# Moving the per-layer embeddings' projections out of the feed-forwards and into the mixers

## The chip, the cores and the metric

The program runs on one core of one Trainium2 chip. The metric is device time in microseconds (us) of one execution of the whole program. Lower is better.

## What is computed

The reference applies two stacks of two layers each to 256 tokens of width 1024. The first stack (feed-forward, mixer, memory attention, feed-forward) is not touched by the change. The second stack does this for its two layers `i`, with `layer_norm` after each step:

```python
h = layer_norm(DN_ALPHA * h + 0.5 * swiglu(h, ffn_w1[i, 0], ffn_w3[i, 0], ffn_w2[i, 0]), ...)
if i % 2 == 0:   # short convolution and state space
    mix = concat([ya, yb]) @ ab_w_out[j]
else:            # sparse attention
    mix = dsa_mixer(h @ c_w_in[j], ...) @ c_w_out[j]
h = layer_norm(DN_ALPHA * h + mix, ...)
h = layer_norm(DN_ALPHA * h + 0.5 * swiglu(h, ffn_w1[i, 1], ffn_w3[i, 1], ffn_w2[i, 1]), ...)
h = h + (p[i] @ ple_w_proj[i]) * jax.nn.sigmoid(h @ ple_w_gate[i])
```

The product `p[i] @ ple_w_proj[i]` is the projection that moves. It is 256 tokens by 256 by 1024, it depends on inputs alone, and it is wanted only in the last line of a layer.

## The kernel before, in words

Tokens are handled in two tiles of 128 (`T` = 0 and 1). Each float32 product is made as three matmuls in a reduced format: high part by high part, high by low, low by high (`mm3`, lines 147 to 152). So each weight that is loaded into a buffer `raw` is split by ScalarE (`whi`, line 126) and VectorE (`wlo`, line 127) before TensorE uses it. There are three `raw`, five `whi` and five `wlo` buffers for the whole program. SyncE's queue issues the weight loads.

A feed-forward (`ffn`, line 293) walks over eleven slices of the hidden width. The last three slices' products with `w_down` form its tail: first all of `T` = 0, then all of `T` = 1. Behind each tile's tail comes `ln_fin`, the layer norm (`L955` to `L578` on VectorE, with one small instruction on GpSimd), and `prep`, which transposes the normalised rows on TensorE (`xT`, `L177`) and splits them into the next stage's operands. The tail of `T` = 1 covers the layer norm of `T` = 0. The layer norm of `T` = 1 is covered by the next stage's matmuls on `T` = 0.

In the second feed-forward of each layer, `pre_tail` calls `ple_proj` (line 964) ahead of the tail. It stages one weight (1 MB), loads each token tile's 128 rows of `p` into one buffer `pn` (`L974`, on ScalarE's DMA queue; `bufs=1`, so the second load waits for the first tile's transposes), transposes and splits them, makes 12 matmuls of 512 columns for each tile, and copies the results to `pr` on VectorE (`L980`). The tiles `pr`, `ph`, `plo` and `pn` are in a pool `pr0` or `pr1` that is opened before that feed-forward and closed after `ple`.

Each stage opens a pool of its own for its working tiles and closes it at its end; the layer norm's gain and bias rows are in that pool too. A stage's pool is laid over the memory of the pool that was closed before it. The state space stage (`ab_mixer`, line 1369) opens a pool, and issues on ScalarE's queue the loads of `NT` (two of 1 MB, `L1380`) and `tab` (768 KB, `L1382`). Then it projects `u` with `proj` (one pass over each token tile, 24 matmuls each) and goes on with products that need both tiles. The sparse attention (`dsa`, line 1000) projects its index queries, then keys and values, then queries, and then runs 16 pairs of head and token tile through scores, softmax, transposes and products with the values.

The framework orders the instructions of each engine when the program is built. An instruction that comes earlier in the program has precedence among those that it takes to be ready, and each engine then runs its own list in order.

Of the kernel before, what the change touches and what calls it, by code (L numbers as in the profile page):

```python
# [29 lines left out]
class Net:  # L30
# [116 lines left out]
    def mm3(self, out, xh, xl, wh, wl, first, last):  # L147
        nc = self.nc
        a, b = ((xl, wh), (xh, wl)) if self.opt("wlast") else ((xh, wl), (xl, wh))
        nc.tensor.matmul(out, xh, wh, start=first, stop=False)  # L150
        nc.tensor.matmul(out, *a, start=False, stop=False)  # L151
        nc.tensor.matmul(out, *b, start=False, stop=last)  # L152

    def both(self, out, ws, x2, n=8, parts=(0, 1)):

# [105 lines left out]
        return [self.stage([(0, w[h * 512:(h + 1) * 512, c0:c0 + width].rearrange("(k p) n -> p k n", p=P))], 4, width)  # L261
                for h in range(2)]

    def proj(self, preps, w, *chunks):

        ws = [self.stage_rows(w, c0, width) for c0, width, _ in chunks]
        for T in range(2):
            xh, xl = preps[T][0:2]
            for wc, (c0, width, cb) in zip(ws, chunks):
                pu = self.psum("A", "proj")  # L270
                for k in range(8):
                    wh, wl = wc[k // 4]
                    self.mm3(pu[:, 0:width], xh[:, k, :], xl[:, k, :], wh[:, k % 4, :], wl[:, k % 4, :], k == 0, k == 7)
                cb(T, pu)

    def out_linear(self, w, lhs, fin, tags=(("C", "C"), ("D1", "D2"))):

        ws = [self.stage([(0, w[i * 256:(i + 1) * 256, :].rearrange("(k p) n -> p k n", p=P))], 2, 1024) for i in range(4)]
        for T in range(2):
            acc = [self.psum(t, "acc") for t in tags[T]]  # L280
            if T and self.opt("halves"):
                order = [(k, n) for n in range(2) for k in range(8)]
            else:
                order = [(k, n) for k in range(8) for n in range(2)]
            for k, n in order:
                h, l = lhs(T, k)
                wh, wl = ws[k // 2]
                s = slice(n * 512, (n + 1) * 512)
                self.mm3(acc[n], h, l, wh[:, k % 2, s], wl[:, k % 2, s], k == 0, k == 7)
            fin(T, acc)  # L290


    def ffn(self, up_parts, w_down, fin, side=None, pooled=False, pre_tail=None, second=None, pieces=1):

        nc, tc = self.nc, self.tc
        (xh, xl), x2 = self.xT_cur, self.x2_cur
# [3 lines left out]
        with tc.tile_pool(name=self.nm("ffn"), bufs=2) as pool:  # L300
# [16 lines left out]
            def stage_down(c):  # L317
                return self.stage([(0, w_down[c * 256:(c + 1) * 256, :].rearrange("(k p) n -> p k n", p=P))], 2, 1024)
# [77 lines left out]
            if side is not None:  # L396
                for _ in side:
                    pass
            if pre_tail is not None:
                pre_tail()  # L400
            its = [(*ht, stage_down(c)) for c, ht in pend]
            for T in range(2):
                for halves in ((0,), (1,)) if T and self.opt("halves") else ((0, 1),):
# [560 lines left out]
    def ple_proj(self, l, pool):  # L964

        nc, a = self.nc, self.a
        pr = [pool.tile([P, D], F32, tag=f"pr{T}", bufs=1, name=self.nm("pr")) for T in range(2)]
        ph = pool.tile([P, 2, 256], F32R, tag="ph", bufs=1, name=self.nm("ph"))
        plo = pool.tile([P, 2, 256], F32R, tag="plo", bufs=1, name=self.nm("plo"))
        wh, wl = self.stage([(0, a["ple_w_proj_2"][l].rearrange("(k p) n -> p k n", p=P))], 2, 1024)  # L970
        for T in range(2):
            s = slice(T * P, (T + 1) * P)
            pn = pool.tile([P, 256], F32, tag="pn", bufs=1, name=self.nm("pn"))
            nc.scalar.dma_start(pn, a["p_2"][l, 0, T * P:(T + 1) * P, :])  # L974
            self.split_T(pn, 2, ph[:, :, s], plo[:, :, s])
            for n in range(2):
                pu = self.psum("A", "pp")
                for k in range(2):
                    self.mm3(pu, ph[:, k, s], plo[:, k, s], wh[:, k, n * 512:(n + 1) * 512], wl[:, k, n * 512:(n + 1) * 512], k == 0, k == 1)
                nc.vector.tensor_copy(pr[T][:, n * 512:(n + 1) * 512], pu)  # L980
        return pr

# [14 lines left out]
            self.out_linear(a["ple_w_gate_2"][l], lambda T, k: (preps[T][0][:, k, :], preps[T][1][:, k, :]), f)  # L997


    def dsa(self, fin):  # L1000
        nc, tc, a = self.nc, self.tc, self.a
        preps = self.preps()
        w_in = a["c_w_in_2"][0]
        with tc.tile_pool(name=self.nm("dsa"), bufs=1) as pl:
# [46 lines left out]
            def cb_q(c):  # L1051
                def cb(T, pu):
                    t = T_([P, 512], "tmp", bufs=2)
                    nc.scalar.activation(t, pu, AF.Copy, scale=128.0 ** -0.5)
                    rot(t.rearrange("p (h d) -> p h d", h=4), 4, T, 16, 16)
                    to_T(t, 4, qT[T][:, 4 * c:4 * c + 4, :])
                return cb
# [31 lines left out]
            for c in range(2):  # L1089
                self.proj(preps, w_in, (c * 512, 512, cb_q(c)))  # L1090

            oh, ol = self.o_tiles()
            for T in range(2):
                nk = P * (T + 1)
# [271 lines left out]
                    nc.sync.dma_start(self.d_mt[:, h, q, :], mt[:, 4 * h:4 * h + 4].rearrange("p g j c -> p (g j c)"))  # L1366


    def ab_mixer(self, fin):
        nc, tc, a = self.nc, self.tc, self.a  # L1370
        preps = self.preps()
        x2 = self.x2_cur
        w_in = a["ab_w_in_2"][0]
        with tc.tile_pool(name=self.nm("ab"), bufs=1) as pl:
# [12 lines left out]
            def cb_u(T, pu):  # L1387
# [3 lines left out]
                for j in range(4):  # L1391
                    nc.tensor.transpose(pt[:, j * P:(j + 1) * P], un[:, j * P:(j + 1) * P], self.ident)
                nc.vector.tensor_copy(uT[:, :, T * P:(T + 1) * P], pt.rearrange("p (k t) -> p k t", k=4))
            self.proj(preps, w_in, (1536, 512, cb_u))


            def projT(c0, cb, ws=None, qs=range(4)):
# [80 lines left out]
            for h in range(2):  # L1478
# [9 lines left out]
                for b in range(4):  # L1488
                    MT = T_([P, 4, P], "MT", bufs=4)
                    nc.sync.dma_start(MT.rearrange("p g m -> p (g m)"), self.d_mt[:, h, b])  # L1490
                    for mm in range(2):
                        n = 4 * b + 2 * h + mm
# [3 lines left out]
                        last = b == 3 and mm == 1  # L1496
# [22 lines left out]
            for q in range(4):  # L1519
                pu = self.psum("A", "glu")  # L1520
# [20 lines left out]
def build(tc, a, out):  # L1541
    with ExitStack() as ctx:
        net = Net(ctx, tc, a, out)
# [59 lines left out]
            net.ffn(net.gu_parts(a["ffn_post_w_gu"][l]), a["ffn_post_w_down"][l], f_next, side=None if l else net.s5_tables())  # L1603
        alpha = 4.0 ** 0.25
        for l in range(2):
            def f_ln(j, mul, eps):
                def f(T, acc, pool, *tags):
                    net.ln_fin(T, acc, mul, eps, l, j, pool, *tags)
                    net.prep(T, rms=False)
                return f  # L1610

            def f_end(T):
                if l == 0:
                    net.prep(T, rms=False)

            def ffn(half, j, **kw):
                net.ffn(net.w13_parts(a["ffn_w1_2"][l, half], a["ffn_w3_2"][l, half]), a["ffn_w2_2"][l, half],
                        f_ln(j, 2 * alpha, 4e-5), pooled=True, **kw)

            net.phase = f"ffn{l}0"  # L1620
            ffn(0, 0)
            net.phase = f"seq{l}"
            (net.ab_mixer if l == 0 else net.dsa)(f_ln(1, alpha, 1e-5))
            net.phase = f"ffn{l}1"
            with tc.tile_pool(name=f"pr{l}", bufs=1) as pp:
                pr = []
                ffn(1, 2, pre_tail=lambda: pr.extend(net.ple_proj(l, pp)))
                net.phase = f"ple{l}"
                net.ple(l, pr, f_end)

# [16 lines left out]
```

## Time and profile before

| | |
|---|---|
| median of 3 runs | 2262.38 us (2260.16 to 2263.03) |
| the profiled execution, its own time | 2264.35 us |
| span of the profiled execution | 2262.4 us |
| mean granted TensorE clock | 0.995 of full speed |
| TensorE matmul busy | 2212.8 us |
| VectorE busy | 1599.5 us |
| ScalarE busy | 1275.1 us |

Times in the views are counted from the span's start. The first feed-forward of layer 0 of the second stack ends and the state space stage begins at about 1430 us. The second feed-forward of that layer ends at about 1724 us. The sparse attention begins at about 1935 us, and the last feed-forward's tail at about 2209 us.

### The profile page before, as it was taken

How to read it: one execution, taken by the hardware profiler on the slowest of the kernel's cores; microseconds unless marked ns; L12 is line 12 of the kernel's file. 1: busy time of each engine (PE TensorE's matmuls, PEld its weight loads, DVE VectorE, ACT ScalarE, POOL GpSimd, SP SyncE). 2: the span in 40 equal slices, each digit the busy share in tenths (PEclk: the TensorE clock that was granted, in tenths of full speed). 3: DMA queues.
4: the chain of work that ended last, by engine and by line, in shares of the span. 5: the costliest groups of instructions: out<-in, count | busy, mean ns of one | idle time of the engine just before them, and what ended most of it. 6: DMA issues, size and time to landing. Idle time of an engine off the chain costs nothing.

```text
span 2262.4 us, 32375 instructions
## 1 busy us (share of the span) xinstructions
PE 2212.8 (98%) x11697; PEld 1844.3 (82%) x11697; DVE 1599.5 (71%) x3522; ACT 1275.1 (56%) x2864; POOL 71.1 (3%) x112
## 2 busy tenths in 40 slices
PE   8999999999999998999999999999999999999998
PEld 6887768788888886777888888787887888778887
DVE  7787666798766776776677565877568565967566
ACT  6745566655655566766555555364555555455553
POOL 0010000000000001100000000000000000000000
PEclk9999999999999999999999999999999999999999
DMA  7665534567577543343655655666555564527552
GB/s 240 228 215 196 191 127 168 161 213 264 177 220 247 173 155 118 130 162 120 200 171 187 223 174 198 219 198 216 185 187 186 187 201 159 166 94 245 186 184 79
DMA packets 280988, 415.94 MB, mean 184 GB/s; under 512 B 18662, under 2 KB 211324, under 8 KB 279804
## 3 DMA queue, kind: packets, MB, share of 16 engines
q1 hardware_dynamic: 275744, 400.87, 53.3%
q10 hardware_dynamic: 5084, 13.00, 1.6%
q8 instruction: 92, 1.51, 0.3%
q14 instruction: 68, 0.56, 0.1%
HBM read 400.07 MB, written 13.76 MB: 183 GB/s over the span
## 4 chain that ended last, share of the span: by engine, by line
PE 79%; DVE 11%; ACT 3%; DMA 2%; issue 2%; POOL 2%; SPq 0%; ACTq 0%; DVEq 0%; POOLq 0%
PE gate L160 11%; PE up L160 11%; PE acc L150 8%; PE acc L151 8%; PE acc L152 8%; PE gate L162 6%; PE up L162 6%; DVE wlo L127 4%; PE proj L151 2%; PE proj L150 2%; PE proj L152 2%; PE up L152 1%; PE up L151 1%; PE up L150 1%; PE xT L177 1%
## 5 line engine op out<-in xcount | busy, mean ns | idle before, releaser
L126 ACT ACTIVATE whi<-raw 128x512 fp32r<-128x512 f32 (+1 forms) x1452 | 816.5, 618 | 413.5 <-PE up L160 176.3
L127 DVE TENSOR_TENSOR wlo<-raw,whi 128x512 fp32r<-128x512 f32 (+1 forms) x1452 | 926.3, 675 | 107.1 <-ACT whi L126 69.6
L160 PE MATMUL gate<-x,whi 128*128 128x512 f32 x1200 | 295.1, 393 | 0.0
L160 PE MATMUL up<-x,whi 128*128 128x512 f32 x1200 | 290.6, 390 | 0.1
L150 PE MATMUL acc<-whi,hh 128*128 128x512 f32 x704 | 276.3, 392 | 2.0 <-ACT hh L192 2.0
L151 PE MATMUL acc<-wlo,hh 128*128 128x512 f32 x704 | 276.4, 393 | 0.0
L152 PE MATMUL acc<-whi,hl 128*128 128x512 f32 x704 | 275.1, 391 | 0.0
L167 DVE TENSOR_TENSOR sg<-gate,sg 128x256 f32<-128x256 f32 x150 | 63.3, 422 | 281.1 <-ACT sg L166 281.1
L160 PEld LDWEIGHTS gate<-x,whi 128*128 128x128 f32 x1200 | 222.2, 189 | 44.1 <-DVE sg L167 0.2
L160 PEld LDWEIGHTS up<-x,whi 128*128 128x128 f32 x1200 | 221.6, 188 | 43.9 <-DVE h L167 0.3
L162 PEld LDWEIGHTS gate<-x,wlo 128*128 128x128 f32 x1200 | 158.2, 191 | 8.3
L162 PE MATMUL gate<-x,wlo 128*128 128x256 f32 x1200 | 160.5, 283 | 0.0
L162 PE MATMUL up<-x,wlo 128*128 128x256 f32 x1200 | 160.5, 283 | 0.0
L162 PEld LDWEIGHTS up<-x,wlo 128*128 128x128 f32 x1200 | 154.9, 191 | 4.5
L150 PE MATMUL proj<-whi,x 128*128 128x512 f32 (+2 forms) x400 | 157.8, 394 | 0.8 <-ACT ti L1032 0.4
L151 PE MATMUL proj<-wlo,x 128*128 128x512 f32 (+2 forms) x400 | 156.4, 391 | 0.0
L150 PEld LDWEIGHTS acc<-whi,hh 128*128 128x128 f32 x704 | 132.9, 189 | 27.9 <-ACT hh L192 2.4
L152 PEld LDWEIGHTS acc<-whi,hl 128*128 128x128 f32 x704 | 132.6, 188 | 28.1 <-DVE hl L193 0.4
L152 PE MATMUL proj<-whi,x 128*128 128x512 f32 (+2 forms) x400 | 154.3, 386 | 0.3 <-DVE x L193 0.3
L151 PEld LDWEIGHTS acc<-wlo,hh 128*128 128x128 f32 x704 | 132.8, 189 | 24.6
L360 ACT ACTIVATE sg<-sg 128x256 f32<-128x256 f32 x150 | 62.5, 417 | 81.0 <-DVE sg L297 79.0
L192 ACT ACTIVATE hh<-h 128x512 fp32r<-128x512 f32 x75 | 47.6, 634 | 104.4 <-DVE h L297 104.4
(732 smaller groups left out, 3007.8 us busy)
## 6 DMA issues: line engine op xcount, KB each, us to landing
raw<-in_ffn_w_dram SPq DMA_DIRECT2D x176, 512.0 KB, 4.7
raw<-in_ffn_post_w_gu_dram SPq DMA_DIRECT2D x88, 512.0 KB, 4.7
raw<-in_ffn_w_dram SPq DMA_DIRECT2D x44, 1024.0 KB, 5.0
raw<-in_ffn_pre_w_gu_dram SPq DMA_DIRECT2D x84, 512.0 KB, 4.9
raw<-in_ffn_pre_w_down_dram SPq DMA_DIRECT2D x22, 1024.0 KB, 5.4
raw<-in_ffn_post_w_down_dram SPq DMA_DIRECT2D x22, 1024.0 KB, 4.9
raw<-in_xmem_wkv_dram SPq DMA_DIRECT2D x16, 1024.0 KB, 4.9
raw<-in_sbg_w_in_dram SPq DMA_DIRECT2D x10, 1024.0 KB, 5.0
```

Of the source, the lines that this page charges most:

```text
L126: self.last_hi = nc.scalar.activation(hi[:, s], raw[:, s], AF.Copy)
L127: self.last_lo = nc.vector.tensor_tensor(out=lo[:, s], in0=raw[:, s], in1=hi[:, s].bitcast(F32), op=ALU.subtract)
L150: nc.tensor.matmul(out, xh, wh, start=first, stop=False)
L151: nc.tensor.matmul(out, *a, start=False, stop=False)
L152: nc.tensor.matmul(out, *b, start=False, stop=last)
L160: mm(out, ws(k)[0], x2[:, k].rearrange("p a t -> p (a t)"), start=k == 0, stop=False)
L162: mm(out[:, 256:512], ws(k)[1], x2[:, k, 0, :], start=False, stop=k == n - 1)
L167: self.nc.vector.tensor_tensor(out=d, in0=ps[:, 256:512], in1=d, op=ALU.add)
L177: nc.tensor.transpose(pt[:, j * P:(j + 1) * P], src[:, (b + j) * P:(b + j + 1) * P], self.ident)
L192: self.nc.scalar.activation(hi, src, AF.Copy)
L360: nc.scalar.activation(d, d, AF.Silu)
```

## The change

`ple_proj` is no longer called in the feed-forwards. In layer 0 it is called in `ab_mixer`, between the two token tiles of the `u` projection (`proj` gets a parameter `between`). The `prep` of token tile 1 behind the feed-forward `ffn00` is taken out of the layer norm's callback (`late`) and put behind `ple_proj`, and its TensorE instructions are ordered after the projection's last matmul (`net.after(net.last_pp)`). In layer 1 `ple_proj` is called in `dsa`, after the last query projection and before the attention. The pools `pr0` and `pr1` are opened before the mixers. The work itself stays the same.

```diff
     def proj(self, preps, w, *chunks, between=None):
...
                 cb(T, pu)
+            if T == 0 and between is not None:
+                between()
...
     def ffn(...):
...
-            if pre_tail is not None:
-                pre_tail()
             its = [(*ht, stage_down(c)) for c, ht in pend]
...
     def ple_proj(...):
...
-                    self.mm3(pu, ph[:, k, s], ...)
+                    self.last_pp = self.mm3(pu, ph[:, k, s], ...)
...
     def dsa(self, fin, other):
...
             for c in range(2):
                 self.proj(preps, w_in, (c * 512, 512, cb_q(c)))
 
+            other()
             oh, ol = self.o_tiles()
...
     def ab_mixer(self, fin, other):
...
-            self.proj(preps, w_in, (1536, 512, cb_u))
+            self.proj(preps, w_in, (1536, 512, cb_u), between=other)
...
-            def f_ln(j, mul, eps):
+            def f_ln(j, mul, eps, late=False):
                 def f(T, acc, pool, *tags):
                     net.ln_fin(T, acc, mul, eps, l, j, pool, *tags)
-                    net.prep(T, rms=False)
+                    if T == 0 or not late:
+                        net.prep(T, rms=False)
...
             ffn(0, 0)
-            net.phase = f"seq{l}"
-            (net.ab_mixer if l == 0 else net.dsa)(f_ln(1, alpha, 1e-5))
-            net.phase = f"ffn{l}1"
             with tc.tile_pool(name=f"pr{l}", bufs=1) as pp:
                 pr = []
-                ffn(1, 2, pre_tail=lambda: pr.extend(net.ple_proj(l, pp)))
+                net.phase = f"seq{l}"
+
+                def other():
+                    pr.extend(net.ple_proj(l, pp))
+                    if l == 0:
+
+                        with net.after(net.last_pp):
+                            net.prep(1, rms=False)
+                (net.ab_mixer if l == 0 else net.dsa)(f_ln(1, alpha, 1e-5), other)
+                net.phase = f"ffn{l}1"
+                ffn(1, 2)
                 net.phase = f"ple{l}"
                 net.ple(l, pr, f_end)
```

## Rows read from the trace of the kernel before

**Rows 1.** Page, part 1: busy time, share of the span, instructions.

```profile
PE 2212.8 (98%) x11697; PEld 1844.3 (82%) x11697; DVE 1599.5 (71%) x3522; ACT 1275.1 (56%) x2864; POOL 71.1 (3%) x112
```

**Rows 2.** Waits of TensorE, whole span: total us, times, longest.

```profile
PE xT L177 <- DVE x L578: 7.3, 10, 1.8
```

**Rows 3.** Timeline of TensorE, state space stage: start, us, instruction, idle before.

```profile
1437.70 1.23 PE L177 MATMUL xT<-ident,x 128*128 128x128 f32 x8 [1.81 <-DVE x L578]
1439.01 0.50 PE L150 MATMUL proj<-whi,x 128*128 128x512 f32 x1
```

**Rows 4.** Timelines of VectorE, GpSimd and ScalarE at the same place.

```profile
1436.87 1.29 DVE L578 TENSOR_TENSOR x<-x,ln_b 128x512 f32<-128x512 f32 x2
...
1438.35 0.11 POOL L1408 MEMSET up<- 128x8 f32 x1 [3.64 <-DMA raw<-in_ab_w_in_dram]
...
1438.42 0.34 ACTq L1380 DMA_DIRECT2D NT<-d_nt  x1
...
1439.36 0.44 ACTq L1382 DMA_DIRECT2D tab<-d_tab  x1
```

**Rows 5.** Timelines of VectorE and ScalarE, start of layer 0's second feed-forward.

```profile
1535.60 1.29 DVE L578 TENSOR_TENSOR x<-x,NO 128x512 f32<-128x512 f32 x2
...
1537.77 0.34 ACTq L974 DMA_DIRECT2D pn<-in_p_dram  x1
1538.14 0.45 ACTq L460 DMA_DIRECT2D ln_g<-in_ln_g_dram  x1
...
1542.17 0.39 ACT L192 ACTIVATE hh<-xT 128x256 fp32r<-128x256 f32 x1 [2.47 <-PE xT L177]
```

**Rows 6.** DMA issues from 1400 to 1470: count, KB each, median us to landing.

```profile
raw<-in_ab_w_in_dram SPq DMA_DIRECT2D x7, 1024.0 KB, 4.9
NT<-d_nt ACTq DMA_DIRECT2D x2, 1024.0 KB, 9.1
...
MT<-d_mt SPq DMA_DIRECT2D x4, 256.0 KB, 10.9
...
tab<-d_tab ACTq DMA_DIRECT2D x1, 768.0 KB
```

**Rows 7.** Tile `pn`, its four loads in the whole span.

```profile
DMA to landing us min/median/max: 1.9/2.8/3.7
```

**Rows 8.** Timeline of TensorE: three tails, first matmul and transposes of tile 0.

```profile
1412.09 0.40 PE L150 MATMUL acc<-whi,hh 128*128 128x512 f32 x1
...
1426.01 1.23 PE L177 MATMUL xT<-ident,x 128*128 128x128 f32 x8 [0.59 <-DVE x L578]
...
1699.95 0.40 PE L150 MATMUL acc<-whi,hh 128*128 128x512 f32 x1
...
1719.94 1.23 PE L177 MATMUL xT<-ident,x 128*128 128x128 f32 x8 [0.58 <-DVE x L578]
...
2209.53 0.40 PE L150 MATMUL acc<-whi,hh 128*128 128x512 f32 x1
...
2229.46 1.23 PE L177 MATMUL xT<-ident,x 128*128 128x128 f32 x8 [0.52 <-DVE x L578]
```

**Rows 9.** Windows at 192 us: us, busy PE, PEld, DVE, ACT, POOL; PEclk, DMA.

```profile
192.00:194.00 2.00, 0.51 (x3) 0.08 (x1) 2.00 (x5) 0.43 (x2) 0.00 (x0) 1.00 1.01 389
194.00:196.00 2.00, 1.54 (x4) 1.02 (x5) 1.04 (x2) 0.41 (x1) 0.00 (x0) 0.68 0.47 66
196.00:198.00 2.00, 2.00 (x6) 1.54 (x6) 0.69 (x1) 0.00 (x0) 0.00 (x0) 0.50 0.86 314
```

**Rows 10.** Windows of the sparse attention, the same columns.

```profile
1995.00:2000.00 5.00, 3.26 (x19) 2.24 (x17) 4.41 (x26) 4.46 (x10) 0.00 (x0) 1.00 0.59 173
2000.00:2005.00 5.00, 4.30 (x15) 3.38 (x16) 3.56 (x23) 3.16 (x13) 0.00 (x0) 0.54 0.28 66
2005.00:2010.00 5.00, 5.00 (x25) 4.22 (x24) 3.62 (x22) 3.44 (x15) 0.00 (x0) 0.78 0.52 182
```

**Rows 11.** Tile `pp`, its copies on VectorE: ns min/median/max, first and last start.

```profile
L980 DVE COPY pr<-pp x8: 680/690/692, 1704.9 to 2218.9; 128x512 f32<-128x512 f32 x8
```

More of the change, by code (lines that the diff above doesn't have):

```diff
@@ L151, in mm3 @@
         nc.tensor.matmul(out, *a, start=False, stop=False)
-        nc.tensor.matmul(out, *b, start=False, stop=last)
+        return nc.tensor.matmul(out, *b, start=False, stop=last)
     def both(self, out, ws, x2, n=8, parts=(0, 1)):
@@ L262, in stage_rows, with proj @@
                 for h in range(2)]
-    def proj(self, preps, w, *chunks):
+    def proj(self, preps, w, *chunks, between=None):
         ws = [self.stage_rows(w, c0, width) for c0, width, _ in chunks]
@@ L290, in out_linear, with ffn @@
             fin(T, acc)
-    def ffn(self, up_parts, w_down, fin, side=None, pooled=False, pre_tail=None, second=None, pieces=1):
+    def ffn(self, up_parts, w_down, fin, side=None, pooled=False, second=None, pieces=1):
         nc, tc = self.nc, self.tc
@@ L978, in ple_proj @@
                 for k in range(2):
-                    self.mm3(pu, ph[:, k, s], plo[:, k, s], wh[:, k, n * 512:(n + 1) * 512], wl[:, k, n * 512:(n + 1) * 512], k == 0, k == 1)
+                    self.last_pp = self.mm3(pu, ph[:, k, s], plo[:, k, s], wh[:, k, n * 512:(n + 1) * 512], wl[:, k, n * 512:(n + 1) * 512], k == 0, k == 1)
                 nc.vector.tensor_copy(pr[T][:, n * 512:(n + 1) * 512], pu)
@@ L997, in ple, with dsa @@
             self.out_linear(a["ple_w_gate_2"][l], lambda T, k: (preps[T][0][:, k, :], preps[T][1][:, k, :]), f)
-    def dsa(self, fin):
+    def dsa(self, fin, other):
         nc, tc, a = self.nc, self.tc, self.a
@@ L1366, in s5_matrices, with ab_mixer @@
                     nc.sync.dma_start(self.d_mt[:, h, q, :], mt[:, 4 * h:4 * h + 4].rearrange("p g j c -> p (g j c)"))
-    def ab_mixer(self, fin):
+    def ab_mixer(self, fin, other):
         nc, tc, a = self.nc, self.tc, self.a
@@ L1617, in ffn @@
                 net.ffn(net.w13_parts(a["ffn_w1_2"][l, half], a["ffn_w3_2"][l, half]), a["ffn_w2_2"][l, half],
-                        f_ln(j, 2 * alpha, 4e-5), pooled=True, **kw)
+                        f_ln(j, 2 * alpha, 4e-5, l == 0 and half == 0), pooled=True, **kw)
             net.phase = f"ffn{l}0"
             ffn(0, 0)
-            net.phase = f"seq{l}"
-            (net.ab_mixer if l == 0 else net.dsa)(f_ln(1, alpha, 1e-5))
-            net.phase = f"ffn{l}1"
             with tc.tile_pool(name=f"pr{l}", bufs=1) as pp:
                 pr = []
-                ffn(1, 2, pre_tail=lambda: pr.extend(net.ple_proj(l, pp)))
+                net.phase = f"seq{l}"
[7 more added lines that the diff above has]
+                ffn(1, 2)
                 net.phase = f"ple{l}"
```

## Prediction

> **What bounds the kernel now.** I read the page's busy times first. TensorE is busy for 2212.8 of 2262.4 us, VectorE for 1599.5 [rows 1]. So some 50 us of TensorE's span are open, and an edit that neither adds nor removes matmuls can only gain by putting work into those open places. Next I read TensorE's waits. Ten waits for the end of a layer norm make 7.3 us in all [rows 2], and the longest, 1.81 us, is where the state space stage wants token tile 1 [rows 3]. Then I read the stretches with a low clock. In the sparse attention's first 15 us TensorE is busy for 3.26, 4.30 and 5.00 of each 5 us, at a granted clock of 1.00, 0.54 and 0.78 [rows 10]. These are the two places into which the projections go. Last I asked when their inputs can be there, from the timelines of the other engines and the DMA issues [rows 4 to 7].
>
> **What is removed.** Two tails lose a projection each. From the first matmul of the tail to the transposes of token tile 0, the tail without projections takes 1426.01 - 1412.09 = 13.92 us; the two with them take 19.99 and 19.93 us [rows 8]. So they lose 6.07 and 6.01 us, together 12.08. What else might end last there, the split weights, is no limit in the tail without projections: its only wait before the transposes is 0.59 us for the layer norm, as in the other two [rows 8]. Leaving the tails also frees VectorE and ScalarE there, which costs and gives nothing, since TensorE sets their pace.
>
> **Layer 0: what is added.** The two tiles' 24 matmuls and four transposes are again about 6.0 us of TensorE. The question is when they can begin. The pool `pr0` is now opened right behind the pool of feed-forward `ffn00`, on the same memory. The rows show what that means. At this seam GpSimd's first write to the new pool comes at 1438.35 and the load of `NT` at 1438.42, just behind the last layer norm instruction of token tile 1, which ends at 1436.87 + 1.29 = 1438.16 [rows 4]. At the next seam the layer norm ends at 1536.89, and the loads of `pn` and of `ln_g`, which nobody wants before the end of that feed-forward near 1719 [rows 8], are issued at 1537.77 and 1538.14 [rows 5]. I read this so: nothing is written into a new pool before the old pool's last user, the layer norm of tile 1, is done. So the load of `pn` can't be issued before 1438.16. That is the moment at which the rows that TensorE waits for are ready anyway (its transposes begin at 1437.70, on the first half of them [rows 3]). The gap is over before the filler can be loaded, and the new order makes the transposes of tile 1, the 24 matmuls behind them and everything later wait for the filler.
>
> How long: on ScalarE's queue `NT`, `NT` and `tab` come first in the program, so `pn` is issued behind `tab`, at 1439.36 + 0.44 = 1439.80 [rows 4]. It then has 2.75 MB ahead of it on its queue, and SyncE's queue carries four loads of `MT` at the same time. The nearest row for a small load in this rush is `MT` itself: 256 KB took 10.9 us, where a whole MB of `raw` takes 4.9 and `NT` took 9.1 [rows 6]. The other bound is `pn` by itself in a quiet stretch, 2.8 us [rows 7]. I take 10.9, because `MT` is in the same rush and of the nearest size: landing at 1450.70. The page "DMA: Bandwidth & Descriptors" of the Trainium skill, section "Queues, rings and completion order", says that each DMA engine takes a queue's descriptors in order, and that a transfer's completion is counted only after all that engine's earlier writes. By that rule `pn` waits for `NT` and `tab`, and the sum is the one below; without it the second rival holds. The row of `MT` agrees with it.
>
> Two transposes take a quarter of the 1.23 us for eight [rows 3], 0.31. Then `pn`'s one buffer is free and the second load goes out, at 1451.0. It lands after 2.8 us (1.9 to 3.7 seen [rows 7]; 10.9 would be the upper bound, but ScalarE's queue is empty then), at 1453.8. Tile 0's projection hides in that wait. Then come two transposes (0.31), a split (0.39 for the same shape [rows 5]) and tile 1's matmuls: (6.07 - 4 x 0.154) / 2 = 2.73 us. They end at 1457.2. From the transposes of `x` to the first matmul on tile 1 it was 1439.01 - 1437.70 = 1.31 us [rows 3]. So tile 1 of `u` begins at 1458.5 instead of 1439.0: 19.5 us later.
>
> TensorE comes out of such a stall at half its clock. After 1.5 us of idling in 192 to 194 the granted clock is 0.68 and 0.50 in the next 4 us [rows 9], a loss of 0.32 x 1.54 + 0.50 x 2.00 = 1.5 us. In the attention it is 0.46 x 4.30 + 0.22 x 5.00 = 3.1 us [rows 10]. Part of it hides in the second wait, so I take 2.0. Layer 0 pays 21.5 us, of which 6.0 are the moved work.
>
> Costed at nothing: the projection's own weight (1 MB, ahead of two weights on SyncE's queue, with its four `whi` and `wlo`) is staged while TensorE idles or works on tile 0. It holds one of five split buffers, so the next product's second weight is split later; the transposes of `u` and that product's first half cover it. Without the cover it would be four pieces of VectorE work, by the copies of the same width [rows 11] an estimated 4 x 0.69 = 2.8 us. Behind the waiting transposes stands all of TensorE's list, and with it ScalarE's copy of `u` and VectorE's transposed copies; none of them can give the time back, since TensorE is full again behind the stall.
>
> **Layer 1.** Here `pn` can be loaded from the seam near 1940 on, some 50 us before it is wanted at 1995, so no wait of that kind arises. The 6.0 us go into the attention. What they can take there is the open time of 1995 to 2005, 1.74 + 0.70 = 2.4 us, and the 3.1 us lost to the low clock, if a busier TensorE keeps it: 5.5 us at most [rows 10]. Against it stand four copies of 0.69 us [rows 11] on a VectorE that is busy for 11.6 of those 15 us [rows 10], and that the projections come first in the program, so that they run ahead of the scores rather than between them. Bounds: 5.5 us back, or 2.8 lost. I take 3.5 back, nearer to the upper end because the clock loss is the larger part. Layer 1 pays 6.0 - 3.5 = 2.5.
>
> **The sum.** -12.08 + 21.5 + 2.5 = +11.9 us. The profiled execution took 2264.35 us, 1.97 more than the median of the runs; it would take 2276.3, and a median of 2262.38 becomes **2274.3 us**.
>
> **Rivals.**
> (a) Small loads are not held up: `pn` lands 2.8 us after its issue, as in the quiet stretches [rows 7]. Then layer 0 pays 8.1 us less, and 1.0 less for the clock: 12.4, in all +2.8, 2265.2 us. For it: `pn` is the smallest transfer here. Against it: `MT` [rows 6].
> (b) The other side: `pn` is loaded and split before the gap, because the pool's first tiles lie on buffers that are free when the tail ends at about 1430. Then the projections fill the gap as written: layer 0 pays 6.07 - 1.81 = 4.3, in all -5.3, 2257.1 us. It decides from the point where the second `pn` is on chip before TensorE's work on tile 0 has run out, at about 1436 to 1438. For it: TensorE's last read of those buffers is early. Against it: [rows 4, 5], where even a tile that nobody hurries for waits for the layer norm.
> (c) Layer 0 as forecast, and the attention gives nothing back and is held up by the copies: +3.5 + 2.8, in all +18.2, 2280.6 us. For it: VectorE there; against it: the low clock, which more work should lift.
>
> **How the numbers follow.** My forecast has a chance of 0.62, (a) 0.19, (b) 0.12, (c) 0.07. What a measurement of this kernel can tell from no change is about 0.2%, 4.5 us. The forecast and (c) are slower by more than that, and 0.03 of (a); (b) is faster for the most part; the rest is no difference: faster 0.12, the same 0.16, slower 0.72. The range leaves out (b) and the far end of (c): 2260 to 2282. The lower end takes in (a) with its clock and attention a little better. The forecast's own range, from the bounds of the attention and 2 us either way for the landings, is 2270 to 2282.
>
> **What would show it.** Right: in the state space stage TensorE idles for more than 10 us between the two tiles of `u`, in two waits, each ended by a load of `pn` or by the split behind it; the load is issued right behind the layer norm; the granted clock falls there; tails of 13.9 us; no projection in them. In the attention less idling and a higher clock between 1995 and 2010, shifted. Wrong: `pn` issued before the layer norm's end, a landing of 3 us, or a gap filled with `pp`.

## The result, and the profile after

The changed kernel takes 2275.49 us (median of 6 runs, 2272.85 to 2279.27) against 2260.87 us for the kernel before on the same chip (6 runs, 2256.73 to 2263.03). The ratio is 1.0068, with a 95% interval of 1.0056 to 1.0080: slower by 14.6 us. The forecast was 2274.3 us with a range of 2260 to 2282.

TensorE's busy time is what it was [rows 1], as the page after shows.

```profile
PE 2211.7 (97%) x11697; PEld 1842.9 (81%) x11697; DVE 1600.5 (70%) x3522; ACT 1275.3 (56%) x2864; POOL 70.9 (3%) x112
```

So the loss is in waits. TensorE's waits over the whole span (total us, times, longest) have two new rows, and one of them leads the list. The layer norms, second here, gave back 1.8 us of the 7.3 before [rows 2]: the wait between the tiles of `u` is gone, as it was meant to be.

```profile
PE xT L177 <- DMA pn<-in_p_dram: 9.9, 1, 9.9
PE xT L177 <- DVE x L578: 5.5, 9, 1.7
...
PE uT L1393 <- ACT un L1390: 4.5, 1, 4.5
```

TensorE's timeline after shows where they stand. Before, the rows after tile 0 of `u` were the transposes of `x` and then tile 1 [rows 3].

```profile
1438.28 1.04 PE L1393 MATMUL uT<-ident,un 128*128 128x128 f32 x4 [4.45 <-ACT un L1390]
1449.26 0.69 PE L177 MATMUL xT<-ident,pn 128*128 128x128 f32 x2 [9.94 <-DMA pn<-in_p_dram]
1450.42 0.79 PE L150 MATMUL pp<-whi,ph 128*128 128x512 f32 x1 [0.47 <-ACT ph L192]
...
1455.61 0.38 PE L177 MATMUL xT<-ident,pn 128*128 128x128 f32 x2
1456.46 0.50 PE L150 MATMUL pp<-whi,ph 128*128 128x512 f32 x1 [0.47 <-ACT ph L192]
...
1459.32 1.03 PE L177 MATMUL xT<-ident,x 128*128 128x128 f32 x8
1460.73 0.50 PE L150 MATMUL proj<-whi,x 128*128 128x512 f32 x1 [0.38 <-ACT x L192]
```

The reader sees two waits one behind the other, 4.45 us for `un` (ScalarE's copy of tile 0 of `u`, which lies in the new pool) and 9.94 us for `pn`. Tile 0's twelve matmuls then take 5.2 us (1450.42 to 1455.61) and tile 1's only 2.9 (1456.46 to 1459.32). The windows of the same stretch (us, busy PE, PEld, DVE, ACT, POOL; PEclk, DMA share, GB/s) tell why: the granted clock is 0.50 for fifteen us.

```profile
1440.00:1445.00 5.00, 0.00 (x0) 0.00 (x0) 0.05 (x1) 0.00 (x0) 0.00 (x0) 0.50 1.00 406
1445.00:1450.00 5.00, 0.69 (x2) 0.29 (x2) 0.00 (x0) 0.01 (x1) 0.00 (x0) 0.50 1.03 404
1450.00:1455.00 5.00, 4.58 (x11) 3.61 (x12) 1.12 (x2) 0.37 (x1) 0.00 (x0) 0.50 0.26 85
1455.00:1460.00 5.00, 4.53 (x24) 3.55 (x23) 2.23 (x4) 0.82 (x2) 0.00 (x0) 0.95 0.00 0
```

ScalarE's timeline after gives the load. The layer norm's last instruction on VectorE starts at 1434.89 here, and the pool opens behind it, as at the two seams before [rows 4, 5].

```profile
1436.27 0.85 ACTq L1381 DMA_DIRECT2D NT<-d_nt  x2
1437.15 0.44 ACTq L1383 DMA_DIRECT2D tab<-d_tab  x1
1437.64 0.58 ACT L1390 COPY un<-proj 128x512 f32<-128x512 f32 x1 [6.97 <-DVE wlo L127]
1442.18 0.34 ACTq L974 DMA_DIRECT2D pn<-in_p_dram  x1
1450.05 0.34 ACTq L974 DMA_DIRECT2D pn<-in_p_dram  x1
```

`pn` is issued behind `tab`, but 4 us behind the copy of `un`, and TensorE gets it 7.1 us after its issue.

**An account by stages.** Each stage ends with TensorE's transposes of tile 0 of `x`. The distances between them make an account that isn't touched by what the execution did earlier: in the trace after, everything ahead of the change runs 2.06 us sooner, by chance. Of the kernel before, these rows stand beside [rows 8]; the first ends the state space stage, the second is a wait early in the feed-forward behind it.

```profile
1526.98 1.26 PE L177 MATMUL xT<-ident,x 128*128 128x128 f32 x8 [1.72 <-DVE x L578]
1551.55 0.44 PE L177 MATMUL xT<-ident,h 128*128 128x128 f32 x2 [2.58 <-DVE h L336]
...
1930.64 1.23 PE L177 MATMUL xT<-ident,x 128*128 128x128 f32 x8 [0.58 <-DVE x L578]
2034.10 1.26 PE L177 MATMUL xT<-ident,x 128*128 128x128 f32 x8 [0.51 <-DVE x L578]
```

And after, with the first matmuls of the two tails:

```profile
1423.95 1.23 PE L177 MATMUL xT<-ident,x 128*128 128x128 f32 x8 [0.58 <-DVE x L578]
...
1548.17 1.26 PE L177 MATMUL xT<-ident,x 128*128 128x128 f32 x8 [1.72 <-DVE x L578]
1571.28 0.44 PE L177 MATMUL xT<-ident,h 128*128 128x128 f32 x2 [1.06 <-DVE h L338]
1719.68 0.40 PE L150 MATMUL acc<-whi,hh 128*128 128x512 f32 x1
...
1733.60 1.23 PE L177 MATMUL xT<-ident,x 128*128 128x128 f32 x8 [0.58 <-DVE x L578]
1944.38 1.23 PE L177 MATMUL xT<-ident,x 128*128 128x128 f32 x8 [0.58 <-DVE x L578]
2050.13 1.26 PE L177 MATMUL xT<-ident,x 128*128 128x128 f32 x8 [0.51 <-DVE x L578]
2226.33 0.40 PE L150 MATMUL acc<-whi,hh 128*128 128x512 f32 x1
2240.18 1.23 PE L177 MATMUL xT<-ident,x 128*128 128x128 f32 x8 [0.52 <-DVE x L578]
```

| stage | before | after | difference | forecast |
|---|---|---|---|---|
| state space stage | 100.97 | 124.22 | +23.25 | +21.5 |
| its second feed-forward | 192.96 | 185.43 | -7.53 | -6.07 |
| next layer's first feed-forward | 210.70 | 210.78 | +0.08 | 0 |
| sparse attention | 103.46 | 105.75 | +2.29 | +2.5 |
| last feed-forward | 195.36 | 190.05 | -5.31 | -6.01 |
| the rest, to the span's end | 32.94 | 32.92 | -0.02 | 0 |
| sum | | | +12.76 | +11.9 |

In the attention the windows that answer to [rows 10] have no low clock any more:

```profile
2005.00:2010.00 5.00, 4.37 (x23) 3.41 (x21) 3.83 (x17) 4.29 (x9) 0.00 (x0) 1.00 0.08 14
2010.00:2015.00 5.00, 4.13 (x20) 3.18 (x21) 4.15 (x18) 4.38 (x11) 0.00 (x0) 1.00 0.70 229
2015.00:2020.00 5.00, 5.00 (x29) 4.09 (x27) 4.25 (x16) 1.49 (x6) 0.00 (x0) 1.00 0.06 12
```

### The profile page after: what moved, and what is told of

It reads as the page before. It is cut to its first block, busy times and chain, and to the rows that moved or that the text cites. A ratio compares the mean times of both kernels' runs of the same rounds, so it can differ in the third digit from the quotient of the medians.

```text
span 2273.1 us, 32375 instructions
## 1 busy us (share of the span) xinstructions
PE 2211.7 (97%) x11697; PEld 1842.9 (81%) x11697; DVE 1600.5 (70%) x3522; ACT 1275.3 (56%) x2864; POOL 70.9 (3%) x112
## 4 chain that ended last, share of the span: by engine, by line
PE 81%; DVE 10%; ACT 4%; DMA 2%; issue 2%; POOL 1%; SPq 0%; ACTq 0%; DVEq 0%; POOLq 0%
PE gate L160 11%; PE up L160 11%; PE acc L152 8%; PE acc L150 8%; PE acc L151 8%; PE gate L162 6%; PE up L162 6%; DVE wlo L127 4%; PE proj L151 3%; PE proj L152 3%; PE proj L150 3%; ACT whi L126 1%; PE up L152 1%; PE up L150 1%; PE up L151 1%
```

## The experiments

All twelve are put together here. "Ratio" is to the kernel before on the same chip, with its 95% interval; the stages are the differences of the account above, each from one profiled execution of its kernel; "`u`" is how much later tile 1 of `u` begins, counted from the transposes of tile 0 of `x` (13.00 us before). The next feed-forward and the rest, within 0.1 us everywhere, are left out of the columns, not of the sum. The second feed-forward's column strays from -6.07 with the wait for `h` at its start, which is 0.73 to 2.98 us in these kernels. In "first in the queue" and in "prepared, `tab` late" it also strays with the clock, which falls soon behind that wait (granted share 0.50 from 1569 to 1571 and 0.51 from 1554 to 1556). The medians stray from the sums by up to 3.7 us, so a sum tells what a stage costs, and the ratio whether the kernel is faster.

| kernel | `u` | state space | its 2nd ffn | attention | last ffn | sum | ratio |
|---|---|---|---|---|---|---|---|
| changed kernel | +23.78 | +23.25 | -7.53 | +2.29 | -5.31 | +12.76 | 1.0068 (1.0056 to 1.0080) |
| attention alone | 0 | +1.14 | -0.80 | +2.32 | -5.49 | -2.80 | 0.9989 (0.9980 to 0.9998) |
| state space alone | +24.13 | +23.61 | -6.56 | +0.17 | +0.05 | +17.34 | 1.0075 (1.0063 to 1.0087) |
| ahead of `tab` | +21.26 | +20.14 | -6.17 | +1.93 | -5.88 | +10.05 | 1.0053 (1.0041 to 1.0066) |
| first in the queue | +15.75 | +15.25 | -3.79 | +2.15 | -5.88 | +7.74 | 1.0042 (1.0030 to 1.0055) |
| first, `tab` last | +13.79 | +12.68 | -6.67 | +2.50 | -5.94 | +2.59 | 1.0025 (1.0015 to 1.0035) |
| early load | +13.65 | +13.14 | -5.82 | +3.62 | -5.70 | +5.34 | 1.0022 (1.0014 to 1.0030) |
| ahead of `u`'s transposes | +13.96 | +14.06 | -7.34 | +4.68 | -5.75 | +5.71 | 1.0022 (1.0013 to 1.0030) |
| own banks | +5.81 | +6.49 | -7.62 | +3.58 | -5.82 | -3.29 | 1.0001 (0.9992 to 1.0010) |
| own banks, `tab` late | +5.82 | +5.02 | -6.27 | +3.19 | -5.72 | -3.70 | 0.9991 (0.9982 to 1.0000) |
| prepared | +4.08 | +8.70 | -6.71 | +5.17 | -5.63 | +1.65 | 1.0022 (1.0013 to 1.0031) |
| prepared, `tab` late | +4.03 | +3.25 | -4.84 | +3.17 | -5.70 | -4.10 | 0.9992 (0.9983 to 1.0001) |
| later | 0 | +6.29 | -6.28 | +3.17 | -6.02 | -2.83 | 0.9997 (0.9988 to 1.0006) |

**Which layer.** Each layer's move alone. The other layer keeps `pre_tail` in its feed-forward.

```diff
 attention alone
-                (net.ab_mixer if l == 0 else net.dsa)(f_ln(1, alpha, 1e-5), other)
+                (net.ab_mixer if l == 0 else net.dsa)(f_ln(1, alpha, 1e-5), proj if l else None)
...
+                ffn(1, 2, pre_tail=None if l else proj)
 state space alone
-            other()            # in dsa
...
+                ffn(1, 2, pre_tail=other if l else None)
```

> Layer 1's projection in the sparse attention, layer 0's back in the tail of its second feed-forward. Theory (the two layers are independent, and the loss is all in layer 0): the last tail loses 5.3 to 6.0 us and the attention pays 2.3 to 2.5 as in the trace after, so 3.0 to 3.5 us faster than before. Rival (the attention gives nothing back, what was seen there is chance): 0 to 3 us slower than before.

> Layer 0's projection between the two tiles of u, layer 1's back in the tail. Theory: layer 0 alone holds the loss, 23.3 us paid in the state space stage less 6.0 to 7.6 given back in the tail: 15.7 to 17.3 us slower than before. Rival (part of the loss is in layer 1 or comes from both together): under 12 us slower.

Measured: 2259.70 against 2262.07 us (-2.4) and 2279.27 (+17.2). The loss is in layer 0 alone. Layer 1's move gains by itself, by about 0.1% (less than the 3.0 to 3.5 us that were expected), with an interval that just leaves out no change. In the state space alone, whose attention is that of before, the low clock in the attention is there again:

```profile
2018.00:2023.00 5.00, 4.63 (x17) 3.46 (x16) 3.57 (x21) 2.91 (x14) 0.00 (x0) 0.50 0.27 80
```

These are the two traces without the projection in the attention, and in both the clock falls there. In the twelve traces with it, it falls in two, and less: the granted clock is 0.73 from 2004 to 2009 in "ahead of `u`'s transposes", and 0.82 and 0.84 in the two windows from 2001 to 2011 in "prepared". So the projection mostly keeps the clock up there.

**The load, taken away.** `pn` gets two buffers in a pool that is opened, and loaded, ahead of the feed-forward before the seam.

```diff
+    def ple_load(self, l, pool):
+        pns = [pool.tile([P, 256], F32, tag=f"pn{T}", bufs=1, ...) for T in range(2)]
+        for T in range(2):
+            self.nc.scalar.dma_start(pns[T], self.a["p_2"][l, 0, T * P:(T + 1) * P, :])
+        return pns
...
             with tc.tile_pool(name=f"pr{l}", bufs=1) as pp:
+                pns = net.ple_load(l, pp) if l == 0 else None
+                net.phase = f"ffn{l}0"
+                ffn(0, 0)
```

> The changed kernel, with both pn of layer 0 in buffers of their own that are opened and loaded ahead of the feed-forward before the seam. Theory (the load is late: new pool, then queue): TensorE waits for un's copy alone, until the new pool opens (4.5 us), then does the 6 us of projection without a wait; tile 1 of u begins some 13 us earlier than in the changed kernel, which makes it 12 to 14 us faster than the changed kernel, about as fast as before. Rival (the projection's weight or its splits, not pn, set the time): 0 to 5 us faster than the changed kernel.

Measured: 2267.08 against 2262.07 us (+5.0). In the stage, 10.1 us of the 23.25 went, not 13. TensorE's rows:

```profile
1436.47 1.12 PE L1403 MATMUL uT<-ident,un 128*128 128x128 f32 x4 [4.72 <-ACT un L1400]
...
1448.52 0.50 PE L150 MATMUL proj<-whi,x 128*128 128x512 f32 x1 [0.38 <-ACT x L192]
```

The wait for `pn` is gone. The wait for `un` stays: the framework put the transposes of `un` ahead of those of `pn` in TensorE's list, and `un` lies in the new pool. The gap passes empty, and from 1436.47 the projection and all else takes 12.05 us, at a granted clock of 0.63 and 0.69 in the two windows from 1435 to 1445. The theory is right in the place, but the late load was less than half of the 23.25 us, and the 12 to 14 us that it promised against the changed kernel came out as 9.6. This kernel takes away two causes at once, the wait for the new pool and the place on the queue; the next runs part them.

**Where the load was late.** Three kernels leave `pn` in the pool that opens at the seam and change its place among the loads. "First in the queue" calls `ple_load` before `ab_mixer`. The other two move `tab` behind the copy of the second `un`, from the changed kernel and from "first in the queue".

```diff
-            nc.scalar.dma_start(tab, self.d_tab)
...
-                nc.scalar.copy(un, pu)
+                cp = nc.scalar.copy(un, pu)
+                if T == 1:
+                    with self.after(cp):
+                        nc.scalar.dma_start(tab, self.d_tab)
```

> The changed kernel, with both pn of layer 0 in buffers of their own, still opened behind the feed-forward before the seam, but issued ahead of NT and tab on ScalarE's queue. Theory (place in the queue is the larger part of the lateness): issued at the opening of the pool, pn lands in 2 to 4 us, about when un's transposes are through, and the time comes within 2 us of the early load: 4 to 7 us slower than before. Rival (the opening of the pools starts so many loads at once that pn is late wherever it stands): 11 to 15 us slower than before, as the changed kernel.

> The changed kernel, with the load of tab moved behind the copy of the second tile of u, so that pn is the eighth load after the seam and not the ninth. In the changed kernel pn's issue came 4.0 us after the instruction before it on ScalarE's queue had ended. Theory (the issue was held until one of eight loads under way had landed): pn is issued right behind un's copy, about 4 us sooner, and lands 3 to 5 us sooner: 3 to 5 us faster than the changed kernel, 9.5 to 11.5 us slower than before. Rival (pn's landing is set by the MBs of NT ahead of it on its queue): it lands when it did, less than 1.5 us off the changed kernel.

> As first in the queue, with tab behind the copy of the second tile of u. There un's copy stood behind tab's issue, and TensorE waited 7.2 us for un. Theory (tab, by then the ninth or tenth load, was held, and held un with it): un's copy comes 2 to 3 us sooner, TensorE waits 4.5 to 5 us for it, and pn is there by then: within 1 us of the early load's stage, 4.5 to 6 us slower than before. Rival (un waits for the pool or for a load of MT, not for the queue): as first in the queue, 8 to 9.5 us slower than before.

Measured: 2270.56 against 2261.64 us (+8.9), 2271.93 (+11.3) and 2266.93 (+6.3) against 2260.66. Ahead of `tab`, ScalarE's and TensorE's rows:

```profile
1436.99 0.42 ACTq L974 DMA_DIRECT2D pn<-in_p_dram  x1
```

```profile
1446.54 0.69 PE L177 MATMUL xT<-ident,pn 128*128 128x128 f32 x2 [7.81 <-DMA pn<-in_p_dram]
```

The issue comes right behind `un`, 5.0 us sooner than in the changed kernel (counted from the transposes of tile 0 of `x`), but the rows only 2.5 us sooner: 9.55 us after issue instead of 7.1. First in the queue with `tab` last:

```profile
1435.84 0.84 ACTq L968 DMA_DIRECT2D pn<-in_p_dram  x2
```

```profile
1438.33 1.11 PE L1405 MATMUL uT<-ident,un 128*128 128x128 f32 x4 [4.93 <-ACT un L1399]
1439.40 1.30 PE L177 MATMUL xT<-ident,pn 128*128 128x128 f32 x3
```

Issued ahead of `NT`, `pn` is there no later than 3.6 us after issue, in the same rush of loads, and TensorE doesn't wait for it. So 9.55 us was the price of standing behind 2 MB on the queue. That it is the order on the queue, and not only the crowd of loads, is seen from the DMA packets of "ahead of `tab`", first from 1437 to 1444 and then from 1444 to 1446.5 (ScalarE's queue is q10, SyncE's q1; packets, millions of bytes, share):

```profile
DMA packets 530, 2.48 MB, mean 355 GB/s; under 512 B 32, under 2 KB 32, under 8 KB 292
q10 hardware_dynamic: 253, 1.94, 69.8%
q1 hardware_dynamic: 276, 0.53, 28.0%
...
DMA packets 511, 0.96 MB, mean 385 GB/s; under 512 B 34, under 2 KB 162, under 8 KB 492
```

A row of `pn` is a packet of 1 KB, and nothing else here has packets from 512 B to 2 KB. In the seven us behind its issue none of them moves, while ScalarE's queue moves 1.94 of the 2.10 million bytes of `NT`; in the next 2.5 us the 128 of the first tile move. In "first, `tab` last" all 256 move before 1440. The rule that the prediction cited, the page "DMA: Bandwidth & Descriptors" of the Trainium skill, section "Queues, rings and completion order", says that an engine takes a queue's descriptors in order; these two runs agree.

In "first in the queue" the wait moved elsewhere. ScalarE's and TensorE's rows:

```profile
1442.35 0.33 ACTq L1393 DMA_DIRECT2D tab<-d_tab  x1
1442.99 0.58 ACT L1400 COPY un<-proj 128x512 f32<-128x512 f32 x1 [9.72 <-DMA MT<-d_mt]
```

```profile
1443.63 1.12 PE L1403 MATMUL uT<-ident,un 128*128 128x128 f32 x4 [7.20 <-ACT un L1400]
```

`tab`'s issue is held, and `un`'s copy stands behind it. With `tab` out of the way TensorE's wait for `un` falls from 7.20 to 4.93 us and the stage reaches the early load's (+12.68 and +13.14), although `pn` waits for the new pool here and not there. So what TensorE paid for `pn` was its place on the queue. The theories of both kernels hold for the landing; their times were missed, that of "first in the queue" by 1.9 us (+8.9 against 4 to 7) and that of "first, `tab` last" by 0.3 (+6.3 against 4.5 to 6). The theory of "ahead of `tab`" holds for the issue and not for the landing. In the changed kernel no packet of `pn` moves from 1437 to 1447, in which time the queue moves 2.79 of the 2.88 million bytes of `NT` and `tab`; its first 128 move from 1447 to 1450. So the 4.0 us by which its issue was held cost nothing there, and the 2.5 us gained are `tab`'s turn on the queue. That is the rival's mechanism, which had counted `NT` alone.

**Filling the gap.** From the early load on: the projection is called ahead of the callback that copies and transposes `un`; then its sums go to other PSUM banks.

```diff
 ahead of u's transposes (in proj)
+                if T == 0 and between is not None:
+                    between()
                 cb(T, pu)
-            if T == 0 and between is not None:
-                between()
 own banks (in ple_proj)
-                pu = self.psum("A", "pp")
+                pu = self.psum("C" if l == 0 else "A", "pp")
```

> As the early load, and the projection is put ahead of un's transposes too, so that nothing in TensorE's list needs the new pool before the projection. Theory: the gap between the two tiles of u is filled from its first us; tile 1 of u begins about 4.5 us later than before the change, and with the two tails and the attention it is 5 to 7 us faster than before. Rival (the weight's last split or VectorE's layer norm holds the projection): no faster than the early load by more than 2 us, so about as fast as before.

> As the projection put ahead of un's transposes, with its sums in the two PSUM banks of the tag C instead of tag A, of which the first tile of u holds one. Theory (one bank makes each product wait for VectorE's copy of the one before, three waits of 0.8 us, and the halved clock that follows doubles the rest): no such wait, the 24 matmuls take 6 to 8 us instead of 15, 7 to 9 us less than without the banks, so 2 to 4 us faster than before. Rival (VectorE, with the layer norm and the splits in the way, sets the time): at most 3 us less than without the banks, 2 us or more slower than before.

Measured: 2267.16 against 2262.07 us (+5.1) and 2262.03 against 2261.64 (+0.4). Ahead of `u`'s transposes the gap is filled from its first us, and nothing is gained. TensorE's rows and windows of that kernel:

```profile
1439.03 0.50 PE L152 MATMUL pp<-whi,plo 128*128 128x512 f32 x1 [1.32 <-DVE plo L193]
...
1441.40 0.80 PE L150 MATMUL pp<-whi,ph 128*128 128x512 f32 x1 [0.78 <-DVE pr L990]
...
1445.21 0.77 PE L150 MATMUL pp<-whi,ph 128*128 128x512 f32 x1 [0.88 <-DVE pr L990]
```

```profile
1440.00:1445.00 5.00, 3.55 (x8) 1.83 (x6) 1.32 (x2) 0.00 (x0) 0.77 (x1) 0.50 1.01 347
```

The split `plo` stands behind the layer norm on VectorE. Behind that wait the clock falls to 0.50. Then each product waits for VectorE's copy of the one before, three times in all (2.44 us), since one of the two banks of tag A still holds tile 0 of `u`, and the matmuls stand 0.43 us apart instead of 0.23. The 24 matmuls take 14.6 us (1436.98 to the transposes of `x` at 1451.62). In the two banks of tag C they take 6.95. The same wait and the window, in own banks:

```profile
1437.51 0.50 PE L152 MATMUL pp<-whi,plo 128*128 128x512 f32 x1 [0.85 <-DVE plo L193]
```

```profile
1440.00:1445.00 5.00, 4.75 (x26) 3.51 (x25) 3.03 (x5) 1.94 (x4) 0.00 (x0) 1.00 0.99 385
```

The three waits are gone, TensorE has four matmuls to do ahead of `plo` instead of two, so that this wait is 0.85 us, and the clock is 1.00 in both windows from 1435 to 1445. Tile 1 of `u` begins 8.2 us sooner in these two traces; the medians differ by 4.7 us only, and the profiled execution of "ahead of `u`'s transposes" was the slowest of its eleven. How much of it is the banks and how much the clock can't be told apart, since both went together. Of the first run the rival was half right (VectorE in the way), and it was no faster than the early load, as the rival had it. Of the second the theory came out for the stage, not for the whole kernel, which is as fast as before and not 2 to 4 us faster.

**Nothing of VectorE ahead of the matmuls.** `pn`'s transposes and splits and the projection's weight are done ahead of the tail before the seam.

```diff
+        for T in range(2):                       # in ple_load
+            s = slice(T * P, (T + 1) * P)
+            self.split_T(pns[T], 2, ph[:, :, s], plo[:, :, s])
+        return ph, plo
...
+                ffn(0, 0, pre_tail=None if l else (lambda: w0.extend(net.ple_weight(0))))
```

> As own banks, and pn's transposes and splits and the staging of the projection's weight are moved ahead of the last products of the feed-forward before the seam, so that between the tiles of u only the 24 matmuls and their copies are left. Theory (with nothing of VectorE ahead of them the matmuls fill the gap from the first us at full clock): tile 1 of u begins 3 to 4 us later than before the change, 5 to 7 us faster than before. Rival (the staging and splits cost as much in the tail as they free): 0 to 2.5 us faster than before, no more than the attention alone.

> As prepared, with tab behind the copy of the second tile of u. There the gap was filled, tile 1 of u began 4.1 us later than before the change, and the stage lost 4.6 us more behind it, where the next product's weight came late. Theory (the loads after the seam fill the DMA engines, and tab's 768 KB take some 2 us of it): 2 us or more of the 4.6 come back, the same as before or up to 2 us faster. Rival (the weight is issued late because its buffers are held, whatever else is loaded): no change to prepared, 1.5 to 5 us slower than before.

> As own banks, with tab behind the copy of the second tile of u. Theory (as there): the wait of 0.8 us ahead of the transposes of u goes, 1 to 2 us less than own banks, 1 to 4 us faster than before. Rival: as own banks, within 1 us.

Measured: prepared 2266.08 against 2261.64 us (+4.4); with `tab` late 2259.87, and own banks with `tab` late 2257.99, both against 2260.66 (-0.8 and -2.7). Prepared does what was expected at the seam (+4.08) and loses 4.6 us behind it, so that neither its theory nor its rival came out in time. TensorE's and ScalarE's rows:

```profile
1457.22 1.36 PE L1456 MATMUL W<-ident,uT 128*128 128x128 f32 x8 [2.98 <-DVE uT L1415]
```

```profile
1455.21 2.19 ACT L126 ACTIVATE whi<-raw 128x512 fp32r<-128x512 f32 x4 [2.98 <-DMA raw<-in_ab_w_in_dram]
```

The next product's weight is late, VectorE waits for its high part, and the copy of `uT`, which has nothing to do with that weight, stands behind. The rest of the 4.6 us is the clock, 0.51 and 0.64 in the two windows from 1458 to 1462. With `tab`'s 768 KB out of the rush the stage costs 5.5 us less (+3.25) and this wait doesn't appear: the theory, and more than its 2 us. In own banks `tab` gives 1.5 us in the stage.

**Another place.** `pn` early, no hold on tile 1, and the projection called ahead of the gated unit.

```diff
-            self.proj(preps, w_in, (1536, 512, cb_u), between=other)
+            self.proj(preps, w_in, (1536, 512, cb_u))
...
+            other()
             gh, gl = self.stage([(0, a["s5_w_glu_2"][0]...)], 4, 512)
```

> pn loaded early, the two tiles of u as before the change, and the projection 65 us later in the state space stage, ahead of the gated unit, where VectorE is busy for 4.35 of 10 us. Theory (it is the place, between the two tiles of u, that costs, not the move): no wait, layer 0 pays 6 us less the 0.8 us of idling there and gets 6.0 to 7.5 back in the tail; with the attention 3 to 5.5 us faster than before. Rival (the projection disturbs the stage wherever it stands): no change or slower.

Measured: 2261.53 against 2261.64 us (ratio 0.9997, 0.9988 to 1.0006). The 6.3 us that the second feed-forward loses, the stage pays: work moved from one full stretch to another. The 0.8 us that TensorE waited there for `z` before are gone, but the transposes of `pn` now wait 0.44 and 0.30 us for ScalarE's copy of `zT`. So the rival came out: no change.

## Why the prediction was right

**The tails.** Forecast -6.07 and -6.01 us. Measured from the first matmul to the transposes, 1733.60 - 1719.68 = 13.92 and 2240.18 - 2226.33 = 13.85, against 19.99 and 19.93 [rows 8]: -6.07 and -6.08. What else changed in those feed-forwards wasn't forecast: -1.46 in the first, where the wait for `h` fell from 2.58 to 1.06 us, and +0.77 in the last, which is spread and wasn't followed.

**The pool.** Right: `pn` isn't loaded before the layer norm's end, and the gap passed empty. But the 10.1 us of the stage that the early load gives back aren't the pool's price. "First, `tab` last", whose `pn` still waits for the pool, gives back 10.6. The pool was paid for through `un`, 4.45 us.

**The landing.** The mechanism was right, a load that waits for what stands ahead of it on its queue, but its numbers agree by luck. Counted from the start of the layer norm's last instruction (1436.87 in [rows 4], 1434.89 after), the issue was forecast at +2.93 us and came at +7.29; the landing was forecast 10.9 us behind it, by `MT`'s row [rows 6], and TensorE had the rows after 7.1. Together 13.83 forecast, 14.37 measured. The two errors cancel, since `pn` moves when `NT` and `tab` are through, whether it is issued 3 or 7 us after that start. And `MT`'s row doesn't bear on that order, as the working says it does: `MT` is on SyncE's queue, with no `NT` ahead of it. Its slowness fits another fact, that the two queues took turns by packets (253 against 276 in the view above) and those of `NT` are larger. That 10.9 us is near the 9.55 us of a load right behind `NT` is chance. What the working calls the second rival is rival (a).

**The signs.** TensorE did idle for more than 10 us between the two tiles of `u`, 14.4, and the clock fell there. But of the two waits one was ended by `un`, not by a load of `pn` or its split, and the load was issued 6.0 us after the layer norm's end, not right behind it.

**The second load and the clock.** Forecast: a second wait of 2.8 us that hides tile 0's projection, and 2.0 us for the clock. There was one wait for a load, not two, since tile 0's matmuls at half clock took 5.2 us and hid the second load. From the first transposes of `pn` to those of `x` it took 10.06 us, where the working had 6.5 + 2.0. With 0.54 from the landing this makes the stage's miss of 1.75 us, less what came back behind `u`.

**What the working lacked.** It took the late load for the whole of layer 0's loss. TensorE would have stood 4.45 us for `un` in any case, and once that wait and the halved clock are counted, a projection whose load is on chip still costs the stage 13.14 us. So rival (b) drew its line in the wrong place: `pn` on chip before the gap, from which it was to decide, is the early load, and its price of 4.3 us for layer 0 was reached only when `un`'s transposes, the PSUM bank and VectorE's work were out of the way too (+5.81 with own banks; +4.08 and +4.03 with `pn` split as well, at `u`). The forecast wasn't hurt by it, since the late load covered all of that. Rival (a), a `pn` that isn't held up, was priced at +2.8 in all; "first, `tab` last" meets its condition, with a sum of +2.59 in its trace and +6.3 us in its median. Rival (c) fell with the attention's +2.29.

**Cover.** The weight's staging, put at nothing with an uncovered price of 2.8 us, was covered in the changed kernel. In prepared, with TensorE no longer waiting at the seam, a late weight cost 2.98 us, and the clock with it.

**Layer 1.** Forecast +2.5 and -6.01, measured +2.29 and -5.31, and the reason that was given, the low clock that more work lifts, is borne out by the state space alone and by most of the traces with the projection there.

**The sum.** The account gives +12.76 in one execution and the medians +14.6, against +11.9. The state space stage is the term that was too small, by 1.75 us. No version tried beats the kernel before by more than 0.11%: the attention alone (0.9989), and the filled gap with `tab` late (0.9991 and 0.9992, whose intervals reach no change). The gap was 1.81 us [rows 3], and the best filling (state space stage and its second feed-forward, 3.25 - 4.84) brings 1.6 of it in its one trace.

## What to carry to other kernels

A gap in front of a layer norm's rows was here a gap of TensorE alone: VectorE is at work on just those rows, and the stage's memory isn't open yet. A filler must have its operands loaded and split, its sums in free banks and its place in the list ahead of anything that waits for the new stage, or it takes the gap's place in the chain. Ask first what the gap holds (here 1.8 us against 6.0 of work), and put small loads that are wanted soon ahead of the large ones on their queue.

## What the runs showed of the hardware

A small load costs what stands ahead of it on its queue: `pn`, 128 KB, took at most 3.6 us first in the queue and 9.55 us behind the two loads of `NT`, in the same rush. From 1437 to 1444 none of its packets moved there, and 1.94 of the 2.10 million bytes of `NT` did.

Two queues that are busy together took turns by packets, not by bytes. From 1437 to 1444 in "ahead of `tab`" ScalarE's queue moved 253 packets and SyncE's 276, but 1.94 against 0.53 million bytes; 238 of the 530 packets had 8 KB or more. So a load in small packets was slow beside one in large packets, also on another queue: `MT` took up to 10.9 us [rows 6].

At this seam eight loads went out one behind the other, and the ninth was held: `pn` by 4.0 us in the changed kernel, `tab` by 1.6 us in "first in the queue". What holds it, whether the program's own bookkeeping of loads or the queue, was not tried. A held issue also held the compute behind it on its engine: `un`'s copy in "first in the queue", for which TensorE waited 7.20 us instead of 4.93. For the load itself it cost nothing in the changed kernel, since its packets couldn't move sooner.

The clock makes small waits large, and not by their length alone. In "ahead of `u`'s transposes" it fell to 0.50 behind a wait of 1.32 us, in "own banks" it stayed at 1.00 behind one of 0.85, and the one wait of 1.81 us at this place [rows 3] left it at 1.00 in the kernel before and in "later", but not in "attention alone", where the first matmul on tile 1 of `u` took 0.80 us instead of 0.50, the granted clock was 0.50 in the next 2 us, and the stage took 1.14 us more with the same work. In the attention the same added work cost 1.93 to 3.62 us where the clock stayed at 1.00, and 4.68 and 5.17 us in the two traces in which it dipped for a while (0.73 over five us, 0.82 and 0.84 over ten).
